# Moving pieces of prompt attention between VectorE, GpSimd and ScalarE, with one rotation and one transposed tile for q and k

## The chip, the cores and the metric

The kernel runs on one core of a Trainium2 chip. The metric is device time in microseconds (us) of one launch, the median of a few runs. TensorE multiplies, VectorE (DVE), ScalarE (ACT) and GpSimd (POOL) do the elementwise work, and SyncE (SP) issues most of the transfers. Each engine works through its own instructions in the order in which the program lists them: an instruction that waits holds up everything behind it on its engine.

## The reference

One inference step of a hybrid decoder layer, in float32: 2048 prompt tokens and 32 sample tokens (8 sequences of 4) of width 1024.

```python
qa, ka, va, qb, kb, vb, ga, gb = _project(x, w_in)
qa, ka, qb, kb = _rope(qa, pos), _rope(ka, pos), _rope(qb, pos), _rope(kb, pos)
# A: 8 query heads on 2 key heads, window 128, with sinks
oa = _band_values(_sink_softmax(_band_scores(qa, ka, 128), sink), va)
# B: three groups of 4 heads; group g reads every 1st, 4th or 16th earlier key
for g, (win, dil) in enumerate(((128, 1), (512, 4), (2048, 16))):
    qg, kg, vg = (_stride_split(z[:, :, hs], dil) for z in (qb, kb, vb))
    p, lse = _softmax_lse(_band_scores(qg, kg, win // dil))
    outs.append(_stride_merge(_band_values(p, vg), n, dil))
ob = _combine_groups(outs, lses)
mix = (sigmoid(ga) * (oa @ w_br_a) + sigmoid(gb) * (ob @ w_br_b)) @ w_o
h = layernorm(ALPHA * x + mix)
u, v = split(h @ w_up)
y = layernorm(ALPHA * h + (gelu(causal_conv3(u)) * v) @ w_down)
```

The sample tokens do the same against cached keys and values. The rotated keys and the values are outputs too.

## The kernel before, in words

**Arithmetic.** TensorE multiplies in a reduced float32 format. To keep float32 accuracy, each operand is split (`split`, lines 40 to 42): ACT copies it to the reduced format (the high half), and DVE, or POOL where the call says so, subtracts that from the original (the low half). A product is then three matmuls: high by high, low by high, high by low.

**Phases.** Phase 1 projects and does all attention; phase 2 merges the branches and applies the first norm; phase 3 is the gated feed-forward. The change lies in phase 1 alone.

**Phase 1.** It runs through five stages: B0, B1, B2 (the three groups of branch B, with strides of 1, 4 and 16 tokens between the rows of a tile), A, and G (the rest of the gates). A stage has 16 prompt tiles of 128 tokens and one sample tile. Each tile has a **slot** (`slot`, line 352): 96 matmuls of 256 columns in two halves, each half into a PSUM tile of the pool `pd`, which has two buffers. A half is four blocks of weights in two steps each, so a slot has eight steps (u, kh). After every step, `adv` lets each pending attention job do its next piece, the newest job first; then the weights of the next stage may be split (`adv_w`), and at steps (1,0) and (3,0) `adv_bg` does one piece of the sample scores.

In a B slot the pieces come so (numbers are steps of the slot after the tile's own projection):

- (0,0): `attn_b` begins. Two transposes of q into a PSUM tile of pool `psT` (three buffers), two of k into one of pool `psO` (one buffer), then `split_q` (ACT L589, DVE L591) and `split_k` (ACT L604 and L606, DVE L608). After it the job before does its last piece: the values of the second pair of heads (L659, into `psT`), their evacuation `both` (ACT L570, DVE L571), an addition on POOL (L662) and a store issued on POOL (L663).
- (0,1): `split_v`. Then `prep`: in B0, `trans_x` transposes the next tile of x through two `psT` tiles (L335) into R, which holds x transposed; in all stages `make_xs` splits the next tile's columns of R (ACT L41, then the low half, L42). In B1 and B2 these columns are read with a stride of 4 or 16 elements.
- (1,0): scores (L617, L619) and `softmax_pair` (line 541): the masked maximum on DVE (L546), its scaling `nm` on DVE (L550), the exponentials on ACT (L552); then a store of maxima and denominators, issued on POOL (L644), which waits for the last exponential. Then `adv_bg`: in `sample_scores` (line 766) DVE multiplies the cached keys by the sample's queries (L797) and sums over the head dimension (L800).
- (2,1): transposes of the first probabilities (L562) and their split (PT, L41 and L42); then, late by design, `evac` of the slot's first half: the rotation `rope` of q and k (L425, L426, L433), which is the last reader of that half's `pd` tile.
- (3,0): the second probabilities; `adv_bg` again, with a product and its sum.
- (3,1): the values of the first pair of heads (L659, into `psO`) and their evacuation.

A tile of a pool is given the buffer that was given out longest ago, and its first writer waits until the last reader of what was there is done. In a B0 slot six `psT` tiles are taken, in this order: q's transposes, the earlier job's values, the two of `trans_x`, and two of transposed probabilities.

In stage A the slot has the same eight steps, `attn_a` has four score tiles per slot, its scaling is at L698, and the low half of the next tile is on POOL already. Products of the sample scores of B0, B1 and B2 run in stages B1, B2 and A: sixteen each, in B1 and B2 two per slot.

What the profile calls `pst` are transposes, `psd` the projections, `pso` values, `xs` the split columns of x, `w` weights, `b` general buffers.

Of the kernel before, what the change touches and what calls it, by code (L numbers as in the profile page):

```python
# [7 lines left out]
F32 = mybir.dt.float32  # L8
F32R = mybir.dt.float32r
AF = mybir.ActivationFunctionType  # L10
ALU = mybir.AluOpType
# [6 lines left out]
NS = 32  # L18
# [6 lines left out]
SCALE = HD ** -0.5  # L25
# [9 lines left out]
class Net:  # L35
# [142 lines left out]
    def phase1(self):  # L178
        nc, tc, a = self.nc, self.tc, self.a
        with ExitStack() as st:  # L180
# [42 lines left out]
            for n, (kind, i, t) in enumerate(seq):  # L223
# [6 lines left out]
                nextp = [q for q in seq[n + 1:n + 3] if q[1] < 16][:1]  # L230
# [9 lines left out]
                def prep():  # L240
                    if kind == "B0" and i + 1 < 16:
                        if i + 2 < 16:
                            self.load_x(i + 2)
                        self.trans_x(i + 1)
                        if i == 0:
                            self.load_xs()
                        if i == 1:
                            self.xs_sample()
                    if nextp and nextp[0][0] != "G" and t[0] == "p":
                        self.load_cs(nextp[0][2][1])  # L250
                    if t[0] == "p" and nextp:
                        return self.make_xs(nextp[0][2], kind == "A")
                    return None

                x2 = self.slot(kind, i, t, xs, units, prep, after_unit, rp)
# [197 lines left out]
    def evac(self, kind, i, t, half, ps):  # L453
        nc, a = self.nc, self.a
        rows = t[1]
        if kind == "G":
            self.gate_out(kind, t, ps, 1024 + half * 512, 512, rows)
            return
        if half == 0:
            cs = self.cs = self.css.pop(0)  # L460
            q = self.at1.tile([128, 512], F32, tag="q", name="q")
            kv = self.at1.tile([128, 512], F32, tag="kv", name="kv")
            self.q, self.kv = q, kv
            if kind == "A":
                self.rope([(q.rearrange("p (r s d) -> p s r d", r=4, s=2), 0, 8)], ps, cs, 128, 8)
            else:
                self.rope([(q[:, 0:256].rearrange("p (h d) -> p h d", d=64), 0, 4),
                           (kv[:, 0:256].rearrange("p (h d) -> p h d", d=64), 4, 8)], ps, cs, 128, 8)
            return
        kv = self.kv  # L470
        if kind == "A":
            self.rope([(kv[:, 0:128].rearrange("p (h d) -> p h d", d=64), 0, 2)], ps[:, 0:128], self.cs, 128, 2)
            self.vr = self.split_v(ps[:, 128:256])
        else:
            self.vps = ps[:, 0:256]
            if kind == "B2" or i == 15 or (kind == "B1" and i % 4 == 3):
                nc.scalar.activation(kv[:, 256:512], ps[:, 0:256], AF.Copy)
            if kind == "B0" and i == 15:
                nc.gpsimd.dma_start(a["cache_b1_p"], kv)
            elif kind == "B1" and i % 4 == 3:  # L480
                nc.gpsimd.dma_start(a["cache_b2_p"][i // 4:i // 4 + 509:4, :], kv)
            elif kind == "B2":
                nc.gpsimd.dma_start(a["cache_b3_p"][rows, :], kv)
        self.gate_out(kind, t, ps[:, 256:512], self.gcol[kind][0] * 256, 256, rows)
        if kind == "A" and i == 15:
            v = self.buf()
            nc.scalar.activation(v[:, 0:128], ps[:, 128:256], AF.Copy)
            nc.gpsimd.dma_start(a["cache_a_p"][:, 0:128], kv[:, 0:128])
            nc.gpsimd.dma_start(a["cache_a_p"][:, 128:256], v[:, 0:128])

    def evac_sample(self, kind, half, ps):
# [9 lines left out]
        if half == 0:  # L501
            self.cs_s = self.at.tile([NS, 128], F32, tag="cs", name="css")
            nc.sync.dma_start(self.cs_s, a["c_rope"][rows, :])
            q = self.at1.tile([NS, 512], F32, tag="q", name="sq")
            kv = self.buf(NS)
            self.q, self.kv = q, kv
            if kind == "A":
# [33 lines left out]
    def softmax_pair(self, sps, nk, mask, m, nm, den, cols, accum=True, init=None):  # L541
# [5 lines left out]
                out=P[:, x, :nk], in0=sps[:, x * 256:x * 256 + nk], in1=mask, scale=1.0,  # L547
                scalar=NEG if init is None else init[:, c:c + 1], op0=ALU.add, op1=ALU.max, accum_out=m[:, c:c + 1])
        csl = slice(cols[0], cols[1] + 1, cols[1] - cols[0])
        nc.vector.tensor_scalar(nm[:, csl], m[:, csl], -SCALE, None, ALU.mult)  # L550
        for x, c in enumerate(cols):
            nc.scalar.activation(P[:, x, :nk], P[:, x, :nk], AF.Exp, bias=nm[:, c:c + 1], scale=SCALE,  # L552
                                 accum_out=den[:, c:c + 1])
# [68 lines left out]
    def attn_b(self, kind, i, t):  # L622
# [3 lines left out]
        sl, mask, nb, swap = self.keys(i, has_prev)  # L626
        nk = nb * 128
        ps = self.psT.tile([128, 512], F32, tag="t", name="pst")
        for p in range(2):
            nc.tensor.transpose(ps[:, p * 128:(p + 1) * 128], q[:, p * 128:(p + 1) * 128], self.idn)  # L630
        qT = self.split_q(ps[:, 0:256].rearrange("p (r t) -> p r t", r=2))
        ps = self.psO.tile([128, 512], F32, tag="o", name="pst")
        for p in range(2):
            nc.tensor.transpose(ps[:, p * 128:(p + 1) * 128], kv[:, p * 128:(p + 1) * 128], self.idn)
        self.split_k(ps[:, 0:256].rearrange("p (r t) -> p r t", r=2), i % 2)
        yield
        v = self.split_v(self.vps)
        vprev, self.vprev = self.vprev, v
# [27 lines left out]
    def attn_a(self, t):  # L666
# [22 lines left out]
        def softmax(r, x, sps):  # L689
# [4 lines left out]
            for y in range(2):  # L694
                nc.vector.tensor_tensor_reduce(out=P[:, y, :nk], in0=sps[x][:, y * 256:y * 256 + nk], in1=mask, scale=1.0,
                                               scalar=self.sk8[:, c + y:c + y + 1], op0=ALU.add, op1=ALU.max,
                                               accum_out=m[:, c + y:c + y + 1])
            nc.vector.tensor_scalar(nm[:, c:c + 2], m[:, c:c + 2], -SCALE, None, ALU.mult)  # L698
            for y in range(2):
                nc.scalar.activation(P[:, y, :nk + 1], P[:, y, :nk + 1], AF.Exp, bias=nm[:, c + y:c + y + 1], scale=SCALE,  # L700
                                     accum_out=den[:, c + y:c + y + 1])
# [64 lines left out]
    def sample_scores(self, g):  # L766
# [25 lines left out]
        for n, (b, th) in enumerate(steps):  # L792
# [1 line left out]
            if n + 1 < len(steps):  # L794
                nxt = load(*steps[n + 1])
            q3 = qb.rearrange("p (t c) -> p t c", t=Kv.shape[1])
            nc.vector.tensor_tensor(q3, Kv, q3, ALU.mult)  # L797
            c0 = b * 4 + th * 2
            dst = self.S[:, g, :, c0:c0 + 2]
            nc.vector.tensor_reduce(dst.rearrange("p h t -> p t h"), qb.rearrange("p (t h d) -> p t h d", t=2, d=64), AX.X, ALU.add)  # L800
# [832 lines left out]
```

## Time and profile before

| | |
|---|---|
| runs | 3258.58, 3260.72 and 3261.48 us, median 3260.72 |
| profiled execution | 3259.99 us, of which the span from first to last instruction is 3258.2 |
| busy | TensorE 3175.0 us (97%), DVE 1947.6 (60%), ACT 1397.0 (43%), POOL 565.5 (17%) |
| stages | B0 to about 280 us, B1 to 535, B2 to 790, A to 1085, G to 1340, phase 2 to 1712, phase 3 to the end |

The span starts with the first instruction. A matmul's row gives its pipelined duration, so consecutive ones overlap. "Idle before" is the time in which an engine stood still before an instruction, with the instruction that ended the wait.

### The profile page before, as it was taken

What the parts mean: (1) busy time and instruction counts of PE and PEld (TensorE: products, weight loads), DVE (VectorE), ACT (ScalarE), POOL (GpSimd) and SP (SyncE); (2) the same over time, 40 slices, a digit from 0 to 9 for tenths busy, and PEclk for the clock granted to TensorE, in tenths of its full rate; (3) what the DMA queues carried; (4) which work ended last, traced back from release to release, by engine and by line L of the source; (5) the groups of instructions that cost most, each with busy time, mean ns of one, the idle gap of its engine ahead of it and who ended that gap; (6) DMA issues with size and microseconds to landing.
All of it is one profiled execution on the core that took longest, in us unless ns stands there. A gap on an engine that the chain in (4) does not pass through costs nothing.

```text
span 3258.2 us, 56718 instructions
## 1 busy us (share of the span) xinstructions
PE 3175.0 (97%) x21839; PEld 2907.4 (89%) x21839; DVE 1947.6 (60%) x4030; ACT 1397.0 (43%) x3097; POOL 565.5 (17%) x671
## 2 busy tenths in 40 slices
PE   8999999999999899899999999999999999999999
PEld 8998999999899899788877988888888888999998
DVE  5667877877887632577765444564446444574446
ACT  6666656665666533412224243342243332342332
POOL 2112112223121200255540000030002100030001
PEclk9999999999999999999999999999999999999999
DMA  3113212412221343876744323443334423443231
GB/s 116 56 47 95 82 31 86 121 63 89 79 57 38 91 131 98 227 194 175 187 131 140 121 84 101 127 142 91 95 100 120 139 86 101 120 138 91 69 95 57
DMA packets 480036, 343.02 MB, mean 105 GB/s; under 512 B 113938, under 2 KB 435564, under 8 KB 479766
## 3 DMA queue, kind: packets, MB, share of 16 engines
q1 hardware_dynamic: 462390, 290.78, 31.5%
q0 software_dynamic: 17232, 48.56, 4.8%
q8 instruction: 172, 2.82, 0.4%
q14 instruction: 98, 0.80, 0.1%
q10 hardware_dynamic: 144, 0.07, 0.0%
HBM read 279.71 MB, written 59.59 MB: 104 GB/s over the span
## 4 chain that ended last, share of the span: by engine, by line
PE 58%; issue 2%; DMA 2%; DVE 1%; SPq 0%; ACT 0%; POOL 0%; DVEq 0%; POOLq 0%; ACTq 0%
PE psu L1392 31%; PE psdn L1070 14%; PE psw L1070 5%; PE psb L1070 4%; PE psd L379 2%; PE psdf L1070 1%; DMA oa<-d_oa 1%; PE pst L1234 0%; PE pso L964 0%; PE pst L1269 0%; DMA ob<-d_ob 0%; DMA ga<-d_gate 0%; DMA b<-in_w_o 0%; SPq L1126 0%; DMA b<-in_w_br_b 0%
## 5 line engine op out<-in xcount | busy, mean ns | idle before, releaser
L1392 PE MATMUL psu<-h,w 128*128 128x512 f32 (+1 forms) x5280 | 1013.6, 354 | 2.2 <-ACT h L41 2.0
L379 PE MATMUL psd<-w,xs 128*128 128x256 f32 x7680 | 1001.1, 285 | 8.7 <-ACT w L41 4.0
L1392 PEld LDWEIGHTS psu<-h,w 128*128 128x128 f32 x5280 | 861.2, 188 | 149.0 <-ACT h L41 3.4
L379 PEld LDWEIGHTS psd<-w,xs 128*128 128x128 f32 x7680 | 945.7, 190 | 12.9 <-ACT w L41 4.4
L1070 PE MATMUL psdn<-w,gt 128*128 128x256 f32 (+1 forms) x4008 | 474.9, 279 | 2.2 <-DVE y L1443 2.2
L1070 PEld LDWEIGHTS psdn<-w,gt 128*128 128x128 f32 (+1 forms) x4008 | 472.2, 186 | 5.3 <-DVE y L1443 4.5
L42 DVE TENSOR_TENSOR w<-b,w 128x512 fp32r<-128x512 f32 (+1 forms) x613 | 403.7, 717 | 21.4 <-ACT w L41 20.4
L41 ACT ACTIVATE w<-b 128x512 fp32r<-128x512 f32 x636 | 346.5, 607 | 127.4 <-PE psdn L1070 64.2
L1403 ACT ACTIVATE ext<-psu 128x512 f32<-128x512 f32 (+1 forms) x110 | 56.3, 512 | 452.2 <-PE psu L1392 452.1
L1416 DVE SCALAR_TENSOR_TENSOR ac<-ext,cw,ac 128x512 f32<-128x512 f32 (+1 forms) x88 | 71.1, 808 | 286.9 <-ACT ac L1415 286.9
L1443 DVE SCALAR_TENSOR_TENSOR y<-y,psdn 128x256 f32<-128x256 f32 x176 | 73.2, 420 | 274.2 <-PE psdn L1070 270.4
L1070 PE MATMUL psw<-WO,mT 128*128 128x512 f32 (+1 forms) x800 | 189.4, 395 | 0.9 <-DVE mT L42 0.9
L1070 PEld LDWEIGHTS psw<-WO,mT 128*128 128x128 f32 (+1 forms) x800 | 148.5, 186 | 38.9 <-DVE mT L42 1.1
L1412 POOL COPY mix<-ext 128x2 f32<-128x2 f32 x66 | 13.0, 196 | 926.5 <-ACT ext L1403 906.4
L42 DVE TENSOR_TENSOR xs<-R,xs 128x1024 fp32r<-128x1024 f32 x64 | 104.8, 1638 | 114.9 <-ACT xs L41 114.8
L1070 PE MATMUL psb<-w,oT 128*128 128x512 f32 (+1 forms) x600 | 147.6, 404 | 7.7 <-ACT b L449 5.0
L41 ACT ACTIVATE gt<-ac 128x512 fp32r<-128x512 f32 x110 | 58.3, 549 | 222.2 <-DVE ac L1423 162.7
L1070 PEld LDWEIGHTS psb<-w,oT 128*128 128x128 f32 (+1 forms) x600 | 112.4, 190 | 36.3 <-ACT b L449 5.7
L552 ACT ACTIVATE P<-P,nm 128x256 f32<-128x256 f32 (+1 forms) x192 | 86.4, 451 | 123.1 <-issue 87.4
L42 DVE TENSOR_TENSOR PT<-pst,PT 128x512 fp32r<-128x512 f32 (+1 forms) x160 | 96.2, 608 | 66.6 <-ACT PT L41 66.0
L662 POOL TENSOR_TENSOR b<-b 64x256 f32<-64x256 f32 x96 | 71.3, 742 | 337.4 <-DVE b L571 337.4
L41 ACT ACTIVATE xs<-R 128x1024 fp32r<-128x1024 f32 x80 | 116.2, 1452 | 0.9 <-ACT b L756 0.4
(257 smaller groups left out, 3679.1 us busy)
## 6 DMA issues: line engine op xcount, KB each, us to landing
b<-in_w_up SPq DMA_DIRECT2D x352, 256.0 KB, 3.9
b<-in_w_down SPq DMA_DIRECT2D x160, 256.0 KB, 3.4
b<-in_w_in SPq DMA_DIRECT2D x80, 256.0 KB, 4.1
b<-in_x_prompt SPq DMA_DIRECT2D x64, 256.0 KB, 4.0
b<-in_cache_b SPq DMA_DIRECT2D x64, 256.0 KB, 3.3
ga<-d_gate SPq DMA_DIRECT2D x32, 512.0 KB, 5.4
b<-d_q SPq DMA_DIRECT2D x48, 256.0 KB, 3.9
d_gate<-b SPq DMA_DIRECT2D x64, 128.0 KB, 1.9
```

The costliest lines, as they stand in the source:

```text
L41: self.nc.scalar.activation(hi, src, AF.Copy)
L42: (eng or self.nc.vector).tensor_tensor(lo, src, hi.bitcast(F32), ALU.subtract)
L379: nc.tensor.matmul(dst, lhsT=l, rhs=r[:, k, :], start=(k == 0 and q == 0), stop=(k == 7 and q == len(ops) - 1))
L552: nc.scalar.activation(P[:, x, :nk], P[:, x, :nk], AF.Exp, bias=nm[:, c:c + 1], scale=SCALE, accum_out=den[:, c:c + 1])
L662: nc.gpsimd.tensor_tensor(o[:, :, 0], o[:, :, 0], o[:, :, 1], ALU.add)
L1070: self.nc.tensor.matmul(ps[:x.shape[1]], lhsT=x, rhs=w, start=(first and q == 0), stop=(last and q == len(ops) - 1))
L1392: nc.tensor.matmul(ps[:, :b1 - b0], lhsT=w[:, k, c0:c0 + 128], rhs=h[:, x, k, b0:b1], start=(k == 0 and q == 0), stop=(k == 7 and q == 2))
L1403: nc.scalar.activation(ext[:, 2 + b0:2 + e1], ps[:, 0:e1 - b0], AF.Copy)
L1412: nc.gpsimd.tensor_copy(carry[:, j, :], ext[:, W:W + 2])
L1416: nc.vector.scalar_tensor_tensor(ac[:, :L], ext[:, 1:1 + L], cw[:, 1, j:j + 1], ac[:, :L], ALU.mult, ALU.add)
L1443: nc.vector.scalar_tensor_tensor(y[x][:M, cs], y[x][:M, cs], ALPHA if first else 1.0, ps[:M], ALU.mult, ALU.add)
```

## The change

1. The low half of the next tile's columns (`make_xs`) is subtracted on POOL when the running slot is of B1, B2 or A; before, of A alone. B0 and G keep it on DVE.
2. In `softmax_pair` and in `attn_a` the scaled maxima `nm` are made by an ACT activation instead of a DVE `tensor_scalar`.
3. In B stages q and k lie side by side in one SBUF tile (`qkv`), and `rope` does both at once: one L425 and one L433 of 512 columns for two of 256 each.
4. In `attn_b` the two transposes of k go into the same `psT` tile as those of q, instead of a `psO` tile. `split_q` and `split_k` both read it.
5. The product of the sample scores (L797) is done on POOL; its sum (L800) stays on DVE.

```diff
-                        return self.make_xs(nextp[0][2], kind == "A")
+                        return self.make_xs(nextp[0][2], kind != "B0" and kind != "G")
...
-            q = self.at1.tile([128, 512], F32, tag="q", name="q")
-            kv = self.at1.tile([128, 512], F32, tag="kv", name="kv")
-            self.q, self.kv = q, kv
+            t = self.at1.tile([128, 1024], F32, tag="qkv", name="qkv")
+            q = t[:, 0:512] if kind == "A" else t[:, 256:512]
+            self.q, self.kv = q, t[:, 512:1024]
...
-                self.rope([(q[:, 0:256].rearrange("p (h d) -> p h d", d=64), 0, 4),
-                           (kv[:, 0:256].rearrange("p (h d) -> p h d", d=64), 4, 8)], ps, cs, 128, 8)
+                self.rope([(t[:, 256:768].rearrange("p (h d) -> p h d", d=64), 0, 8)], ps, cs, 128, 8)
...
-            q = self.at1.tile([NS, 512], F32, tag="q", name="sq")
+            q = self.at1.tile([NS, 1024], F32, tag="qkv", name="sq")[:, 0:512]
...
-        nc.vector.tensor_scalar(nm[:, csl], m[:, csl], -SCALE, None, ALU.mult)
+        nc.scalar.activation(nm[:, csl], m[:, csl], AF.Copy, scale=-SCALE)
...
-        for p in range(2):
-            nc.tensor.transpose(ps[:, p * 128:(p + 1) * 128], q[:, p * 128:(p + 1) * 128], self.idn)
+        for p in range(4):
+            nc.tensor.transpose(ps[:, p * 128:(p + 1) * 128], (q, kv)[p // 2][:, p % 2 * 128:(p % 2 + 1) * 128], self.idn)
         qT = self.split_q(ps[:, 0:256].rearrange("p (r t) -> p r t", r=2))
-        ps = self.psO.tile([128, 512], F32, tag="o", name="pst")
-        for p in range(2):
-            nc.tensor.transpose(ps[:, p * 128:(p + 1) * 128], kv[:, p * 128:(p + 1) * 128], self.idn)
-        self.split_k(ps[:, 0:256].rearrange("p (r t) -> p r t", r=2), i % 2)
+        self.split_k(ps[:, 256:512].rearrange("p (r t) -> p r t", r=2), i % 2)
...
-            nc.vector.tensor_scalar(nm[:, c:c + 2], m[:, c:c + 2], -SCALE, None, ALU.mult)
+            nc.scalar.activation(nm[:, c:c + 2], m[:, c:c + 2], AF.Copy, scale=-SCALE)
...
-            nc.vector.tensor_tensor(q3, Kv, q3, ALU.mult)
+            nc.gpsimd.tensor_tensor(q3, Kv, q3, ALU.mult)
```

## The prediction

> **What bounds the kernel now.** I read the stretches first: busy time of each engine by stage. Columns: stretch, its length, busy us (instructions) of TensorE, its weight loads, DVE, ACT and POOL, then granted clock, DMA share, GB/s. The rows are B0, B1, B2 and A.
>
> ```profile
> 12.00:280.00 268.00, 263.05 (x2200) 260.37 (x2198) 171.80 (x441) 166.45 (x409) 51.91 (x72) 0.99 0.24 74
> 280.00:535.00 255.00, 240.25 (x1978) 232.00 (x1976) 192.29 (x456) 153.72 (x369) 50.13 (x71) 1.00 0.21 64
> 535.00:790.00 255.00, 244.34 (x1974) 237.19 (x1975) 195.41 (x484) 155.82 (x401) 63.28 (x89) 0.97 0.31 94
> 790.00:1085.00 295.00, 286.58 (x2294) 270.49 (x2294) 233.05 (x597) 177.04 (x533) 60.73 (x48) 1.00 0.22 60
> ```
>
> TensorE sets the time everywhere: DVE is at most 79% busy. All that the change can win is TensorE's idle time in these stages: 5, 15, 11 and 8 us, plus late starts of weight loads. So the waits of TensorE, stage by stage, are next (us in total, times, longest): B1, then B2, then A.
>
> ```profile
> PE pst L634 <- DVE b L571: 6.9, 9, 0.9
> PE psd L379 <- DVE b L426: 1.8, 1, 1.8
> ...
> PEld pst L562 <- ACT P L552: 7.9, 20, 0.9
> ```
>
> ```profile
> PE pst L634 <- DVE b L571: 4.6, 9, 0.5
> PE psd L379 <- DVE b L426: 1.6, 1, 1.6
> ...
> PEld pst L562 <- ACT P L552: 3.1, 10, 0.4
> ```
>
> ```profile
> PE pso L713 <- DVE PT L42: 3.6, 14, 0.3
> PE pst L678 <- DVE kv L433: 2.5, 5, 0.6
> ```
>
> Three causes: k's transposes wait for the one `psO` buffer (L634), those of the probabilities for late exponentials (L562), and at a stage's first slot the projection waits for the rotation to free its `pd` buffer (L379 behind L426).
>
> **Gains.** (1) With k in q's tile the wait for `psO` goes: 6.9 + 4.6 = **11.5 us**. (2) The low half of x stands on DVE ahead of the maxima; without it the exponentials come about 2 us earlier, and only ACT's own high half is ahead of them. The L562 waits go; they show at the weight loads (7.9 + 3.1 = 11.0), a part of which lies under the matmul before. Between 0 and 11.0 I take **8 us**, near the top because these loads stand right ahead of TensorE's next work. (3) The same low half delays the first rotation of B1 and of B2; off DVE, 1.8 + 1.6 = **3.4 us** go. (4) In A, DVE loses a product per step (the L797 row below) and the scaling, which POOL's low half holds up in every slot:
>
> ```profile
> 899.32 1.40 DVE L698 TENSOR_SCALAR nm<-m 128x2 f32<-128x2 f32 x1
> ```
>
> ```profile
> L693 ACT ACTIVATE P<-sk 128x2 f32<-128x2 f32 x64 | 12.6, 196 | 0.0
> ```
>
> On ACT a form of the same size takes 0.196 us (L693), so the scaling costs ACT 0.2 us, is no longer held, and the exponentials of A come about 1.2 us earlier. A's two waits, 3.6 + 2.5 = 6.1 us, are mostly covered; I take **5.5 us** (bounds 0 and 6.1). (5) The rotation at once issues two instructions fewer per tile, but consecutive DVE instructions overlap (starts 0.33 us apart, below), so it gains under 0.1 us per tile, and none of it ends a wait of TensorE: 0. The 160 scalings on ACT, 0.2 us each, lie under ACT's 38% idle in these stages: 0. Sum: 11.5 + 8 + 3.4 + 5.5 = **28.4 us**.
>
> **A loss in B0.** In each B0 slot six `psT` tiles are taken on three buffers, so the second tile of `trans_x` gets the buffer of q's transposes. Its last reader is now L591; with k in the same tile it becomes L608, the last part of `split_k`. One slot of B0 (start, duration):
>
> ```profile
> 138.34 0.86 DVE L591 TENSOR_TENSOR qT<-pst,qT 64x256 fp32r<-64x256 f32 x2 [1.07 <-ACT qT L589]
> ...
> 139.50 1.03 PE L335 MATMUL pst<-idn,b 128*128 128x128 f32 x8
> 139.93 0.87 DVE L608 TENSOR_TENSOR kL<-pst,kH 64x256 fp32r<-64x256 f32 x2 [0.73 <-ACT kH L606]
> ```
>
> L591 ends at 139.20; the fifth of the eight transposes, the first into the second tile, starts at 139.93 without a wait. L608 ends at 140.80, and a handoff from DVE to TensorE takes 0.06 us (669.98 + 0.67 to 670.71 below), so this transpose could start at 140.86: TensorE stands still for 0.93 us, in a slot that has no idle time to absorb it. L608 can't come earlier, since ACT's L606 ends its wait. Slots 2 to 14 of B0 have the same order: 13 x 0.93 = **12.1 us**. Bounds: 0, if the wait is kept by columns rather than by buffer, and 13 x 1.14, if ACT's first copy waits for all four transposes, two more of about 0.1 us each (1.03 for eight).
>
> **A new wait in B1 and B2.** In a slot with a product, POOL's order becomes: store of values (L663), low half of x, store of maxima (L644, which waits for the exponentials), product. DVE's order is: sum L800, then PT, then the rotation. So the sum stands on DVE waiting for POOL, and PT and the rotation behind it; and the rotation's L426 frees the `pd` buffer of the next slot's first matmul. A slot of B2:
>
> ```profile
> 669.98 0.67 DVE L571 TENSOR_TENSOR b<-pso,b 64x512 f32<-64x512 f32 x1
> ...
> 670.71 0.44 PE L634 MATMUL pst<-idn,kv 128*128 128x128 f32 x2 [0.52 <-DVE b L571]
> ...
> 673.71 2.01 ACT L41 ACTIVATE xs<-R 128x1024 fp32r<-128x1024 f32 x1
> ...
> 675.39 0.73 POOL L663 DMA_DIRECT2D d_ob<-b  x1 [0.30 <-POOL b L662]
> ...
> 678.97 0.69 DVE L797 TENSOR_TENSOR b<-b 128x512 f32<-128x512 f32 x1
> 679.69 0.69 DVE L800 TENSOR_REDUCE S<-b 128x8 f32<-128x512 f32 x1
> 680.38 0.56 POOL L644 DMA_DIRECT2D d_md<-md  x1 [4.27 <-ACT PT L41]
> 680.39 0.42 DVE L42 TENSOR_TENSOR PT<-pst,PT 128x256 fp32r<-128x256 f32 x1
> 680.73 0.41 DVE L425 TENSOR_TENSOR q<-psd,cs 128x256 f32<-128x256 f32 x1
> 681.06 0.41 DVE L425 TENSOR_TENSOR kv<-psd,cs 128x256 f32<-128x256 f32 x1
> 681.39 0.68 DVE L426 TENSOR_TENSOR b<-psd,cs 128x512 f32<-128x512 f32 x1
> 682.83 1.58 PE L379 MATMUL psd<-w,xs 128*128 128x256 f32 x12
> ```
>
> Durations on POOL, contiguous and strided on DVE (B0, B1, A on POOL, and a POOL `tensor_tensor` of the product's size; min/median/max):
>
> ```profile
> L42 DVE TENSOR_TENSOR xs<-R,xs x16: 1224/1226/2029, 24.6 to 251.3; 128x1024 fp32r<-128x1024 f32 x16
> L42 DVE TENSOR_TENSOR xs<-R,xs x14: 1961/2032/2048, 312.2 to 514.0; 128x1024 fp32r<-128x1024 f32 x14
> L42 POOL TENSOR_TENSOR xs<-R,xs x15: 2382/2394/2409, 802.9 to 1069.5; 128x1024 fp32r<-128x1024 f32 x15
> L1221 POOL TENSOR_TENSOR m<-ga x34: 1267/1303/1642, 1344.1 to 1693.5; 128x512 f32<-128x512 f32 x32, 32x512 f32<-32x512 f32 x2
> ```
>
> The product is 1.30 us. The low half takes 2.39 on POOL contiguous; strided by 4 or 16 elements it is unknown, call it d. DVE pays 2.03 - 1.23 = 0.80 for the stride. Bounds: 2.39 (POOL too slow to notice) and 2.39 x 2.03 / 1.23 = 3.95; I take the same addition as DVE's, **3.2**, since it is the same operation on the same memory.
>
> Then: POOL is free at 675.39 + 0.73 = 676.12 (ACT's high half ends at 675.72). Low half, store, product and sum with three handoffs: 676.12 + d + 0.56 + 1.30 + 0.69 + 0.18 = 678.85 + d. PT (0.34 to the next start), L425 (0.66), L426 (0.68) and the handoff: 680.59 + d. The next slot's matmul, now at 682.83, would come at 682.31 without the 0.52 us at L634. Wait: **d - 1.72**. The exponentials aren't the limit: the store that waits for them stands at 680.38 now, they come about 2 us earlier, and POOL's low half ends at 679.3.
>
> A B1 slot with two key blocks has a longer PT and more work on TensorE. From one without a product, whose L562 wait (0.66, and 0.93 - 0.60 in the four transposes) goes too:
>
> ```profile
> 496.42 2.08 ACT L41 ACTIVATE xs<-R 128x1024 fp32r<-128x1024 f32 x1
> 498.08 0.73 POOL L663 DMA_DIRECT2D d_ob<-b  x1 [0.29 <-POOL b L662]
> 502.19 0.93 PE L562 MATMUL pst<-idn,P 128*128 128x128 f32 x4 [0.66 <-ACT P L552]
> 504.12 0.69 DVE L42 TENSOR_TENSOR PT<-pst,PT 128x512 fp32r<-128x512 f32 x1 [1.79 <-ACT PT L41]
> 504.39 0.60 PE L562 MATMUL pst<-idn,P 128*128 128x128 f32 x4
> 506.71 1.58 PE L379 MATMUL psd<-w,xs 128*128 128x256 f32 x12
> ```
>
> 498.81 + d + 2.73, then 0.61 + 0.66 + 0.68 + 0.06, is 503.55 + d against 505.72: **d - 2.17**. Sixteen slots hold products: six of B1 with two key blocks, two with one, eight of B2 with one. At 3.2: 6 x 1.03 + 10 x 1.48 = **21.0 us**; at 2.39: 8.0; at 3.95: 33.0.
>
> [...]
>
> **The sum.** 12.1 + 21.0 - 28.4 = +4.7 us on the profiled execution's own 3259.99 us (span 3258.2, 1.8 around it): **3265 us**. That execution lies 0.7 under the median of the runs, 3260.72. 0.2% is 6.5 us, what a measurement here tells from no change: 3265 counts as the same.
>
> **Rivals.**
>
> *The stride costs POOL nothing* (d = 2.39). For it: POOL needs 2.39 us where DVE needs 1.23, so its reads may have slack. Against: ACT and DVE both pay. New wait 8.0: 12.1 + 8.0 - 28.4 = -8.3, **3252 us**.
>
> *B0 does not wait*: the second tile of `trans_x` finds its buffer free. For it: nothing in the trace shows this reuse, since no wait falls there now. Against: L634's wait for L571 shows that a PSUM buffer waits for its last reader. 3265 - 12.1 = **3253 us**.
>
> *The chain on POOL is longer still*, the case that ends slower: in the sixteen slots POOL pays for the stride in DVE's proportion, d = 3.95; new wait 33.0, sum +16.7, **3277 us**. It makes the kernel slower than the measurement's 0.2% from d = 3.3 on.
>
> *POOL's product shuts out the rotation's second half.* A DVE operation stood still for as long as POOL's low half ran (L698, 1.40 us). The second product (1.30 us) ends, by the times above, about 1 us before the rotation's additions L433 begin. If it ran 1.3 us later, L433 and q's transposes behind it would be late by up to 0.5 us in sixteen slots: +8, **3273 us**. [...]
>
> **How the numbers follow.** Chances: forecast (d from 2.9 to 3.6, 3260 to 3271) 0.42; no cost of the stride 0.20; no wait in B0 0.13; longer chain 0.15; rotation shut out 0.10. The forecast's 0.42 is same 0.30 and slower 0.12; the two rivals at 3252 and 3253 are faster for two thirds (0.22) and same for the rest (0.11); the last two are slower (0.25). So faster 0.22, same 0.41, slower 0.37. The range, 3247 to 3281, spans the rivals with some 4 us beyond, for the takes of 8 and 5.5.
>
> **What would show it.** B0: TensorE waiting at L335 for L608, about 0.95 us in 13 slots, and slots of 16.4 us; without it the loss is wrong. B1 and B2: no wait at L634 nor L562; in slots with products a wait at L379 for L426 of 1 to 1.5 us, and DVE idle ahead of L800 until POOL. The strided low half on POOL: 3.2 us; 2.4 or 4 decides between the cases. A: slots about 0.3 to 0.9 us shorter. If the L379 wait is absent though d is over 3, the order I read from the queues is wrong.

## The result and the profile after

The changed kernel takes 3304.68 us (median; 3299.81 to 3306.83) beside 3261.10 (3258.58 to 3261.72) of the kernel before on the same chip: a ratio of 1.0133, 95% interval 1.0115 to 1.0151. It is 44 us slower; the prediction was 3265, with a range up to 3281. Its profiled execution took 3304.76 us (span 3303.0).

The stretches of the changed kernel first, cut at the same distances from each stage's first transposes of q as those shown of before, to within a microsecond (length, busy time and instructions of TensorE, weight loads, DVE, ACT, POOL; granted clock, DMA share, GB/s):

```profile
12.00:320.00 308.00, 273.07 (x2196) 267.08 (x2196) 164.95 (x376) 174.16 (x440) 51.95 (x71) 0.97 0.21 65
320.00:581.70 261.70, 249.72 (x1984) 237.37 (x1982) 142.48 (x361) 160.79 (x402) 117.54 (x103) 1.00 0.21 62
581.70:855.60 273.90, 253.22 (x1973) 239.71 (x1974) 147.62 (x389) 163.47 (x434) 129.41 (x121) 0.99 0.28 88
855.60:1133.60 278.00, 276.42 (x2296) 270.47 (x2297) 195.17 (x521) 187.78 (x593) 81.51 (x64) 1.00 0.23 64
```

TensorE, idle for 5 us of B0 before, now stands still for 35 us there, and its clock is 0.97. In A it is hardly idle at all. From the first transposes of q of one stage to those of the next (start times in the trace; A to those of its sixteenth tile), the stages of the profiled executions are:

| us | B0 | B1 | B2 | A | the rest |
|---|---|---|---|---|---|
| before | 262.9 | 262.6 | 243.7 | 282.6 | 2206.4 |
| changed | 303.7 | 269.2 | 262.7 | 265.6 | 2201.8 |
| difference | +40.8 | +6.6 | +19.0 | -17.0 | -4.6 |

What TensorE waits for in B0 of the changed kernel (us in total, times, longest; "issue" means that the profile names nothing that ended the wait):

```profile
PE pst L335 <- issue: 25.7, 13, 2.2
...
PE pst L343 <- ACT R L336: 2.0, 1, 2.0
```

The wait that the prediction foretold for B0 is there, 13 times, but it is 1.96 us long instead of 0.93. One such slot (start, duration):

```profile
157.63 0.60 PE L629 MATMUL pst<-idn,qkv 128*128 128x128 f32 x4
158.27 0.77 ACT L588 ACTIVATE qT<-pst 64x256 fp32r<-64x256 f32 x2 [0.85 <-PE pst L629]
...
159.07 0.86 DVE L590 TENSOR_TENSOR qT<-pst,qT 64x256 fp32r<-64x256 f32 x2 [1.29 <-ACT qT L588]
...
159.96 0.77 ACT L603 ACTIVATE kH<-pst 64x256 fp32r<-64x256 f32 x2 [0.93 <-DVE qT L590]
...
160.74 0.78 ACT L605 ACTIVATE kH<-pst 64x256 fp32r<-64x256 f32 x2
161.55 0.86 DVE L607 TENSOR_TENSOR kL<-pst,kH 64x256 fp32r<-64x256 f32 x2 [1.63 <-ACT kH L605]
...
162.51 0.63 PE L335 MATMUL pst<-idn,b 128*128 128x128 f32 x4 [1.95 <-issue]
```

L335 starts 0.10 us after L607, the last reader of the buffer, has ended (161.55 + 0.86 = 162.41). The row to see is ACT L603. It copies k out of the shared tile and needs nothing of `qT`, yet it waits 0.93 us until DVE has subtracted q's low half (L590: 159.07 + 0.86 = 159.93). So ACT and DVE read the tile (the expectations call it a bank) in turns: ACT q, DVE q, ACT k, DVE k. The turns are kept by semaphores of the program: in the trace this L603 waits for the one that the second L590 raises. In the slot of before that the prediction shows, ACT's first copies of k waited for TensorE's semaphore alone and ran beside DVE's L591 (138.34):

```profile
137.12 0.38 PE L630 MATMUL pst<-idn,q 128*128 128x128 f32 x2
...
138.33 0.77 ACT L604 ACTIVATE kH<-pst 64x256 fp32r<-64x256 f32 x2
```

There k's low half ended 3.68 us after the transposes began (140.80 - 137.12); now it is 4.78 (162.41 - 157.63), and the buffer is free only then. It is so in all 48 B slots; for L603 the trace has this wait (us, times):

```profile
  DVE qT L590: 44.9, 48
```

In B1 (first list) and B2 (second) it shows at the scores, whose weight loads (PEld) wait for k's halves (L616, L618):

```profile
PE psd L379 <- DVE b L426: 4.9, 8, 0.8
...
PEld pss L618 <- DVE kL L607: 8.6, 32, 0.3
PEld psd L379 <- PE pso L655: 6.3, 8, 1.0
...
PEld pss L616 <- ACT kH L605: 2.5, 8, 0.9
```

```profile
PE psd L379 <- DVE b L426: 6.3, 8, 0.8
...
PEld pss L618 <- DVE kL L607: 8.6, 32, 0.3
PEld psd L379 <- PE pso L655: 8.0, 9, 1.0
...
PEld pss L616 <- ACT kH L605: 5.0, 18, 1.1
```

The waits for `psO` at k's transposes and those for late exponentials (L634 and L562 of before) are gone from both lists, as foretold. In their place stand the scores' 24.7 us (8.6 + 2.5 + 8.6 + 5.0) and, in slots with a product, the wait at L379. Such a slot of B1:

```profile
436.35 2.91 POOL L42 TENSOR_TENSOR xs<-R,xs 128x1024 fp32r<-128x1024 f32 x1
...
439.20 0.56 POOL L640 DMA_DIRECT2D d_md<-md  x1
439.77 2.55 POOL L793 TENSOR_TENSOR b<-b 128x512 f32<-128x512 f32 x2
...
441.11 0.69 DVE L796 TENSOR_REDUCE S<-b 128x8 f32<-128x512 f32 x1 [4.87 <-POOL b L793]
441.71 0.68 DVE L42 TENSOR_TENSOR PT<-pst,PT 128x512 fp32r<-128x512 f32 x1
...
442.91 0.68 DVE L426 TENSOR_TENSOR b<-psd,cs 128x512 f32<-128x512 f32 x1
443.73 1.66 PE L379 MATMUL psd<-w,xs 128*128 128x256 f32 x12 [0.56 <-DVE b L426]
```

The chain is the predicted one, link by link: low half, store, product, sum, PT, rotation, matmul. The strided low half takes 2.91 us where the prediction took 3.2.

### The profile page after: what moved, and what is told of

Same layout as the page of the kernel before. It is cut to its first block, busy times and chain, and to the rows that moved or that the text cites. A ratio compares the mean times of both kernels' runs of the same rounds, so it can differ in the third digit from the quotient of the medians.

```text
span 3303.0 us, 56625 instructions
## 1 busy us (share of the span) xinstructions
PE 3192.0 (97%) x21839; PEld 2921.9 (88%) x21839; DVE 1804.3 (55%) x3694; ACT 1430.3 (43%) x3257; POOL 721.8 (22%) x751
## 4 chain that ended last, share of the span: by engine, by line
PE 60%; DMA 1%; DVE 1%; issue 1%; ACT 0%; POOL 0%; SPq 0%; DVEq 0%; ACTq 0%; POOLq 0%
PE psu L1388 30%; PE psdn L1066 14%; PE psw L1066 5%; PE psb L1066 4%; PE psd L379 4%; PE psdf L1066 1%; DMA oa<-d_oa 1%; PE pso L960 1%; PE pst L1230 0%; PE pst L1265 0%; DMA ob<-d_ob 0%; DVE w L42 0%; DMA b<-in_w_o 0%; DVE y L1439 0%; DMA b<-in_w_br_a 0%
## 5 line engine op out<-in xcount | busy, mean ns | idle before, releaser
L379 PE MATMUL psd<-w,xs 128*128 128x256 f32 x7680 | 1004.4, 285 | 19.9 <-DVE b L426 11.5
L379 PEld LDWEIGHTS psd<-w,xs 128*128 128x128 f32 x7680 | 946.9, 190 | 27.4 <-PE pso L655 14.3
L41 ACT ACTIVATE PT<-pst 128x512 fp32r<-128x512 f32 (+1 forms) x160 | 84.3, 536 | 124.3 <-PE pst L561 123.4
L42 POOL TENSOR_TENSOR xs<-R,xs 128x1024 fp32r<-128x1024 f32 x48 | 132.3, 2757 | 22.9 <-ACT xs L41 13.3
```

The lines of the kernel that those rows point to most:

```text
L41: self.nc.scalar.activation(hi, src, AF.Copy)
L42: (eng or self.nc.vector).tensor_tensor(lo, src, hi.bitcast(F32), ALU.subtract)
L379: nc.tensor.matmul(dst, lhsT=l, rhs=r[:, k, :], start=(k == 0 and q == 0), stop=(k == 7 and q == len(ops) - 1))
```

## The experiments

Each ratio is against runs of the kernel before on the same chip. Stage lengths are worked out as in the table above, from one profiled execution each; what lies outside the four stages comes to between 2201.0 and 2212.4 us there, so sums over the stages differ from differences of the medians by up to some 7 us.

| kernel | us, median | ratio, 95% interval | B0 | B1 | B2 | A |
|---|---|---|---|---|---|---|
| changed, k in its own tile again | 3234.60 | 0.9920 (0.9905 to 0.9935) | 262.2 | 253.8 | 245.2 | 265.6 |
| before, k in q's tile alone | 3328.27 | 1.0208 (1.0192 to 1.0223) | 304.3 | 277.8 | 261.2 | 282.7 |
| changed, ACT's copies first | 3261.87 | 1.0006 (0.9997 to 1.0015) | 281.3 | 256.3 | 249.9 | 265.6 |
| changed, x through the scores' tile | 3288.25 | 1.0084 (1.0068 to 1.0101) | 283.0 | 269.2 | 262.9 | 265.7 |
| changed, x through the values' tile | 3275.45 | 1.0047 (1.0030 to 1.0064) | 270.3 | 269.1 | 263.5 | 265.6 |
| changed, product on DVE | 3288.21 | 1.0084 (1.0069 to 1.0100) | 303.7 | 261.0 | 251.5 | 266.1 |
| before, product on POOL alone | 3294.15 | 1.0109 (1.0094 to 1.0124) | 262.9 | 276.0 | 262.1 | 284.5 |
| the same, store of maxima on ACT | 3270.26 | 1.0031 (1.0020 to 1.0042) | 263.9 | 266.2 | 251.8 | 284.2 |
| before, low half on POOL alone | 3244.95 | 0.9951 (0.9937 to 0.9966) | 262.1 | 254.2 | 237.8 | 283.0 |
| before, scaling on ACT alone | 3247.30 | 0.9957 (0.9940 to 0.9973) | 263.0 | 264.1 | 245.4 | 266.1 |
| changed, k own tile, product on DVE | 3222.12 | 0.9886 (0.9871 to 0.9900) | 262.2 | 250.3 | 236.5 | 266.2 |
| changed, k in a scores' tile, product on DVE | 3222.03 | 0.9881 (0.9865 to 0.9897) | 262.0 | 247.2 | 237.3 | 266.2 |

**1. k back in its own tile**, the rest of the change as it is.

```diff
-        for p in range(4):
-            nc.tensor.transpose(ps[:, p * 128:(p + 1) * 128], (q, kv)[p // 2][:, p % 2 * 128:(p % 2 + 1) * 128], self.idn)
+        for p in range(2):
+            nc.tensor.transpose(ps[:, p * 128:(p + 1) * 128], q[:, p * 128:(p + 1) * 128], self.idn)
         qT = self.split_q(ps[:, 0:256].rearrange("p (r t) -> p r t", r=2))
-        self.split_k(ps[:, 256:512].rearrange("p (r t) -> p r t", r=2), i % 2)
+        ps = self.psO.tile([128, 512], F32, tag="o", name="pst")
+        for p in range(2):
+            nc.tensor.transpose(ps[:, p * 128:(p + 1) * 128], kv[:, p * 128:(p + 1) * 128], self.idn)
+        self.split_k(ps[:, 0:256].rearrange("p (r t) -> p r t", r=2), i % 2)
```

> The changed kernel, with k's transposes back in their own psO tile and all else kept. Bank theory: B0 as before the change, the scores of B1 and B2 no longer wait for k, stage A keeps its gain of 17 us; what is left of the loss is the rotation behind the sum in the sixteen slots with products, 10 to 16 us by the forecast's formula with the measured 2.9 us low half; 3240 to 3258 us. POOL theory: only the 12 us of B0 come back; about 3292 us.

Measured: 3234.60, 70 us below the changed kernel and 0.8% below the one before, better than the 3240 to 3258 expected. B0, B1 and B2 lose 41.5, 15.4 and 17.5 us, 74.4 together. Two rows of its B0 show ACT's copies of k and DVE's subtraction of q starting together again:

```profile
138.36 0.77 ACT L603 ACTIVATE kH<-pst 64x256 fp32r<-64x256 f32 x2
138.37 0.86 DVE L590 TENSOR_TENSOR qT<-pst,qT 64x256 fp32r<-64x256 f32 x2 [1.07 <-ACT qT L588]
```

So the tile that q and k share costs more than the whole loss; the other four parts together are a gain.

**2. The shared tile alone**, put into the kernel before (the edit is the first one's reverse).

> The kernel before, with only the two transposes of k moved into the PSUM tile of q. Bank theory (ACT and DVE read one PSUM bank only in turn, so splitting q and splitting k run one after the other, k's low half comes 1.1 us later in each B slot, and in B0 the second tile of x waits for it about 2 us in 13 slots): B0 longer by 35 to 42 us as in the changed kernel, the waits for the psO buffer (11.5 us) gone in B1 and B2 but scores and exponentials about 0.6 us later there; 3290 to 3310 us. POOL theory (the loss comes from the queue of low half, store, product and sum): B0 longer by my predicted 12 us at most, B1 and B2 shorter by 11; 3262 us.

Measured: 3328.27, worse than expected by either theory. Against before, B0, B1 and B2 gain 41.4, 15.2 and 17.5 us, 74.1 together. These are the same sizes as in the first experiment, so the expectation's discount for the other parts was wrong: over the stages the shared tile costs 74 us whether they are there or not (by the medians 70 there and 67 here). TensorE waits 25.7 us at L335 here too, the same as in the changed kernel, which clears POOL for B0.

**3. ACT's copies first.** q and k stay in one tile and in the same buffers; ACT copies both high halves before DVE subtracts, and k's second copies come from SBUF.

```diff
         for x, here, there in self.HALF:
             nc.scalar.activation(qT[x][here, :n], q3[here], AF.Copy)
-        for x, here, there in self.HALF:
-            nc.vector.tensor_tensor(qT[x][there, :n], q3[here], qT[x][here, :n].bitcast(F32), ALU.subtract)
...
         for x, here, there in self.HALF:
             nc.scalar.activation(self.kH[x][here, :n, cur], k3[here], AF.Copy)
         for x, here, there in self.HALF:
-            nc.scalar.activation(self.kH[x][there, :n, cur], k3[here], AF.Copy)
+            nc.scalar.activation(self.kH[x][there, :n, cur], self.kH[x][here, :n, cur].bitcast(F32), AF.Copy)
+        for x, here, there in self.HALF:
+            nc.vector.tensor_tensor(qT[x][there, :n], q3[here], qT[x][here, :n].bitcast(F32), ALU.subtract)
         for x, here, there in self.HALF:
             nc.vector.tensor_tensor(self.kL[x][here, :n, cur], k3[here], self.kH[x][here, :n, cur].bitcast(F32), ALU.subtract)
```

> The changed kernel, q and k in one bank and in the same buffers; only the order in the splits differs: ACT copies the high halves of q and k out of the bank first (four reads), takes k's second copies from SBUF, and DVE then does its four subtractions. So the bank changes hands once instead of three times. Bank theory: DVE's first subtraction starts about 0.8 us later than now (after ACT's fourth read), but k's low half ends about 1.2 us earlier; the wait at L335 falls from 25.7 to some 10 us, the half-clock stretches of B0 go, the waits of L616 and L618 for k fall to under 5 us: B0 275 to 285, total 3265 to 3280. Rival (k is late for another reason, and ACT and DVE may read one bank at once): DVE's subtraction of q starts right behind ACT's copies of q as now, k's low half gains under 0.3 us: 3300 to 3306.

Measured: 3261.87, 43 us below the changed kernel by the order of ten small instructions and the source of two, and the same as before. A slot of its B0 (L606 are the first copies of k, L608 those from SBUF, L611 and L613 the subtractions):

```profile
145.15 0.60 PE L635 MATMUL pst<-idn,qkv 128*128 128x128 f32 x4
145.78 0.77 ACT L588 ACTIVATE qT<-pst 64x256 fp32r<-64x256 f32 x2 [0.85 <-PE pst L635]
146.57 0.78 ACT L606 ACTIVATE kH<-pst 64x256 fp32r<-64x256 f32 x2
147.25 0.84 ACT L608 ACTIVATE kH<-kH 64x256 fp32r<-64x256 f32 x2
...
147.38 0.86 DVE L611 TENSOR_TENSOR qT<-pst,qT 64x256 fp32r<-64x256 f32 x2 [2.09 <-ACT kH L606]
...
148.25 0.86 DVE L613 TENSOR_TENSOR kL<-pst,kH 64x256 fp32r<-64x256 f32 x2
...
149.21 0.63 PE L335 MATMUL pst<-idn,b 128*128 128x128 f32 x4 [1.14 <-issue]
```

L611 subtracts q and has its operands at 146.55, but starts at 147.38, when ACT has read k out of the same tile (146.57 + 0.78 = 147.35): the rival, by which both read it at once, falls. L608, which reads SBUF, runs beside L611 (147.25 to 148.09, and from 147.38). The low half of k ends 3.96 us after the transposes began (4.78 in the changed kernel), a gain of 0.82, not the expected 1.2. The wait at L335 falls to 1.14 us, 15.0 in all where some 10 were expected, and those of the scores' weight loads for k in B1 and B2 from 24.7 to 6.8 in all. The total is below the expected 3265 to 3280.

**4. Which part of B0's loss is the late buffer?** The second tile of `trans_x` is taken elsewhere, so L335 has nothing to wait for; q and k keep sharing. First from the scores' pool, then from the values'.

```diff
-            ps = self.psT.tile([128, 512], F32, tag="t", name="pst")
+            ps = (self.psS if h else self.psT).tile([128, 512], F32, tag="s" if h else "t", name="pst")
```

> The changed kernel, with one edit: the second of the two tiles in which trans_x transposes the next tile of x (stage B0 alone) comes from the pool of the scores, so it no longer needs the buffer in which q and k lie. q and k stay in one bank. It tells apart two parts of B0's loss of 41 us: the buffer handed on late (L335 behind L607) and k's late low half as such. Theory 1 (most of B0 is the buffer): the 25.7 us at L335 go, the slots lose their 2.1 us and the half-clock windows with them, B0 comes to 265 to 275, B1 and B2 stay at 269 and 263: 3304.8 - 34 = about 3270 (3266 to 3277). Theory 2 (B0's loss is the late k; the wait at L335 only stands where the scores would wait otherwise): scores then wait at L616 and L618, B0 stays above 285: 3287 or more.

Measured: 3288.25, which lies in the second theory's range; B0 283.0, which neither theory gave. The wait at L335 is gone, but a new one took its place, because the scores' second buffer now waits for the copy of x out of it:

```profile
PE pss L616 <- ACT R L336: 15.1, 14, 1.4
```

So the run doesn't decide. The second, with `psO` and tag "o" in place of `psS` and "s":

> The changed kernel; the second tile of trans_x (B0 alone) comes from the pool of the values (psO), which stands empty at that time. q and k stay in one bank. With the scores' pool the wait at L335 went, but 15.1 us came at L616, behind the copy of x out of the scores' buffer (B0 283.0). Here nothing should come in its place. Theory 1 (B0's loss is the buffer handed on late, and the half clock that its waits bring): B0 263 to 267, 3264 to 3270. Theory 2 (k's late low half costs B0 something of its own): B0 270 to 283, 3271 to 3287. B1 and B2 stay at 269 and 263 by both.

Measured: 3275.45; B0 270.3, and no wait took the old one's place. Both numbers lie in the second theory's ranges, B0 at their lower edge, yet both theories hold a share: 33.4 us of B0 go with the buffer, and 7.4 over before's 262.9 stay with the late k. Slots of B0 here last 15.88 us, against 15.47 in the first experiment, with hardly any idle time of TensorE; the row that differs is the weight loads' wait for the probabilities, 6.8 us in all (0.8 in the first experiment):

```profile
PEld pst L561 <- ACT P L551: 6.8, 27, 0.8
```

**5. Product back on DVE**, otherwise the changed kernel.

```diff
-            nc.gpsimd.tensor_tensor(q3, Kv, q3, ALU.mult)
+            nc.vector.tensor_tensor(q3, Kv, q3, ALU.mult)
```

> The changed kernel, with the product of the sample scores back on DVE. If the waits of the projection for the rotation come from the sum that stands behind POOL's product: they go (11 us of TensorE idle, and about 1.2 us per B2 slot with products), B1 and B2 shorter by 12 to 18 us, 3286 to 3293 us. If they come from the low half of x on POOL or from k's bank alone: within 3 us of 3305 us.

Measured: 3288.21, 16.5 us less, as expected (B1 8.2, B2 11.2); the waits at L379 behind L426 are gone. In the weight loads' rows they came to 14.3 us (the rows that name L655 above: 6.3 and 8.0), now 0.4; the wait of the values for PT, on the same chain, falls from 10.8 to 5.1. Together these fell by 19.6 us, close to the 19.4 by stages.

**6. Product on POOL alone**, in the kernel before: does it cost anything without the low half ahead of it?

> The kernel before with the fifth part alone: the product of the sample scores on POOL, the low half of x on DVE. By the prediction's chain, wait = d - 1.72 with d = 0 on POOL: no new wait at L379; the store of maxima, later by the low half's 2 us on DVE, adds some: 3259 to 3264. Rival: the product costs what it cost beside POOL's low half (12 to 16 us), since POOL and DVE hold each other up in SBUF: 3270 or more.

Measured: 3294.15, a miss: it costs 34 us, twice as much as in the changed kernel (B1 +13.4, B2 +18.4). A slot of B2:

```profile
592.23 0.56 POOL L644 DMA_DIRECT2D d_md<-md  x1 [4.20 <-ACT PT L41]
592.85 2.52 POOL L797 TENSOR_TENSOR b<-b 128x512 f32<-128x512 f32 x2
...
594.17 0.69 DVE L800 TENSOR_REDUCE S<-b 128x8 f32<-128x512 f32 x1 [3.36 <-POOL b L797]
...
596.60 1.66 PE L379 MATMUL psd<-w,xs 128*128 128x256 f32 x12 [0.85 <-DVE b L426]
```

POOL stands idle for 4.20 us at the store of the maxima, and the product behind it (the row names PT, ACT's next instruction; the last exponential ends at 591.94). With the low half on DVE the exponentials that the store waits for come late. I had put d = 0 into the prediction's sum and forgotten that the store then sets the time.

**7. The same, with the store of the maxima issued on ACT.**

```diff
-        nc.gpsimd.dma_start(self.d_md[g, rows, :], md)
+        nc.scalar.dma_start(self.d_md[g, rows, :], md)
```

> The kernel before with the product on POOL (which alone gave 3294) and one edit more: the store of maxima and denominators is issued on ACT, right behind the exponentials that it waits for, instead of on POOL ahead of the product. Theory 1 (the product is late because that store stands ahead of it on POOL and waits 4 to 5 us for the exponentials, and the sum on DVE waits for the product): the wait of DVE at L800 (56.5 us in B1 and B2) falls under 10, the waits at L379 behind L426 go, B1 and B2 come back to 263 and 244 or some us less, 3254 to 3264. Theory 2 (POOL's product, two operands from SBUF, holds DVE up by itself, or is held up): the loss stays above 12 us in B1 and B2, 3272 or more.

Measured: 3270.26, between the two ranges. DVE's wait at the sum is gone altogether, as the first theory says, and 20 of the 32 us with it. B1 and B2 still stand 3.6 and 8.1 over before, which the second theory explains in kind:

```profile
593.34 1.96 DVE L42 TENSOR_TENSOR xs<-R,xs 128x1024 fp32r<-128x1024 f32 x1 [0.97 <-ACT xs L41]
...
593.84 3.80 POOL L797 TENSOR_TENSOR b<-b 128x512 f32<-128x512 f32 x2
...
596.88 0.79 DVE L550 TENSOR_SCALAR nm<-md 128x2 f32<-128x2 f32 x1
```

Freed of the store, the pair of products (2.52 us above) starts during DVE's low half (first row) and takes 3.80, and the scaling of a 128x2 tile takes 0.79 us, not the 0.17 that it takes before (mean of 32 in B2: 0.453 against 0.172). This one ends at 597.67, POOL's pair at 597.64. It is so for all 32 scalings of B1 and B2 that took over 0.3 us here: each ends 0.02 to 0.03 us after one of POOL's products. So the two engines held each other up in these slots (3.80 us for 2.52, 0.79 for 0.17), and the exponentials wait for the scaling. That this is all of the 11.7 us left was not tried; the edit has a price of its own, since ACT computes nothing for up to 0.40 us around the issue of the store (0.33), which comes to 11.2 us in B1 and B2.

**8. The low half on POOL alone**, in the kernel before.

```diff
-                        return self.make_xs(nextp[0][2], kind == "A")
+                        return self.make_xs(nextp[0][2], kind != "B0" and kind != "G")
```

> The kernel before with the first part alone: the low half of the next tile's columns on POOL in B1 and B2. Products stay on DVE, k in its own tile. By the gains as the prediction sized them (waits at L562, 11.0 us, of which 8; the first rotations, 3.4) B1 and B2 are about 11 us shorter: 3250 (3248 to 3252). Rival: the waits at L634 and L562 are one chain, and what is saved at L562 comes back at L634, since the values that free the buffer come no earlier: under 4 us, 3257 to 3261.

Measured: 3244.95, better than the 3248 to 3252 expected; B1 and B2 lose 8.4 and 5.9 us. The rival falls.

**9. The scaling on ACT alone**, in the kernel before (the change's second part).

> The kernel before, with only the scaling of the maxima moved to ACT. If A's gain of 17 us comes from the scaling that stood behind POOL's low half: A shorter by 10 to 17 us, B stages within 2 us, 3244 to 3251 us. If it comes from DVE losing the products: A shorter by 5 us at most, 3256 us or more.

Measured: 3247.30, as expected for a gain in A: A loses 16.5 us, B1 and B2 nothing (+1.5, +1.7). The weight loads of A before, and below of this run, show where it sat (L562 is gone from the second list):

```profile
PEld pso L713 <- DVE PT L42: 9.6, 27, 0.5
PEld pst L562 <- ACT P L700: 7.7, 29, 0.5
PEld pst L678 <- DVE kv L433: 3.7, 5, 0.8
```

```profile
PEld pso L713 <- DVE PT L42: 3.1, 13, 0.2
...
PEld pst L678 <- DVE kv L433: 1.5, 5, 0.4
```

The three rows fall from 21.0 us to 4.6, by 16.4. In the kernel before, 15 of A's scalings took 0.84 to 1.89 us, and each ended 0.02 to 0.04 us after POOL's low half; on ACT the scaling waits for POOL no longer.

**10. Without the two parts that cost**: k in its own tile and the product on DVE; then the same with k's transposes in a tile of the scores' pool, as stage A does it.

> The changed kernel with k's transposes back in their own tile (as in the run that gave 3234.6) and the product back on DVE. If the product on POOL costs what it cost beside the shared bank (16.5 us, there with 12.6 us of waits of L379 behind L426), this comes to 3218 to 3222. If with its own bank only the waits at L379 matter (6.5 us in that run), 3226 to 3230.

> The changed kernel with k's transposes in a tile of the scores' pool, as stage A does it, and the product on DVE. q and k in separate banks, and no wait for the one buffer of the values' pool (L633 behind L570, 6.7 us with k there). If that buffer is all that is left between this and the run with k in the values' pool: 5 to 7 us below that one, 3212 to 3222. Rival: the scores' tiles are reused by k, so that the scores of the next pair of heads wait for split_k or k waits for the maxima and exponentials of the job before: then no better than that run, 3220 to 3235.

Measured: 3222.12 and 3222.03, 1.1 to 1.2% faster than the kernel before. Taking the product off POOL is worth 12.5 us here by the medians (12.2 by stages), more than its waits at L379 (6.5) and less than the 16.5 beside the shared tile. The two kernels can't be told apart: the wait for `psO` goes (B1 is 3.1 us shorter), but with k in the scores' pool the total is no better, and 3222 is where the first expected range ends and inside the rival's. The trace shows the rival's first wait: in B1 and B2 the scores' weight loads (L616) wait 6.5 us in all there, where k's transposes waited 9.2 us with k in its own tile.

## Why the prediction was wrong

By its own steps, in us over the stages B0 to A:

| term | predicted | measured | from |
|---|---|---|---|
| k in q's tile: B0, less the waits at L634 | 12.1 - 11.5 = +0.6 | +74.4 | experiment 1 |
| product on POOL behind the low half | +21.0 | +12.2 | experiment 10, first run, to experiment 1 (B1 3.5, B2 8.7) |
| low half off DVE (8 + 3.4) | -11.4 | -14.3 | experiment 8 |
| A | -5.5 | -17.0 | stage table |
| scaling, one rotation in B1 and B2 | 0 | -5.2 | experiment 8 to the first run of 10 (the scaling alone: +3.2) |
| B0 without the shared tile | 0 | -0.7 | before to experiment 1 |
| sum, B0 to A | +4.7 | +49.4 | stages: 40.8 + 6.6 + 19.0 - 17.0 = 49.4 |

With -4.6 in the other stages this is the +44.8 between the profiled executions. The rows are steps of one path from before to the changed kernel, so they add up by their making; rows of a few us, the scaling's and the 4.6 among them, may be no more than the difference between single executions. The terms depend on the kernel in which they are measured: beside the shared tile the product costs 19.4 (experiment 5), in the kernel before 31.8 (experiment 6).

**The step that failed** is the term for k in q's tile: the sentence "L608 can't come earlier, since ACT's L606 ends its wait", and the sum built on it, which leaves L608 where it was; only the upper bound of 1.14 asks whether it comes later. It replayed the splits as they ran in two tiles, q's subtraction on DVE beside k's copies on ACT. In one tile they take turns. That makes k's low half 1.1 us later (4.78 us after the first transposes instead of 3.68). The wait in B0 was 1.96 us instead of 0.93; the term, put at +0.6 us with the gain at L634, measured +74.4. My upper bound of 13 x 1.14 allowed 0.2 us for two more transposes and nothing for the reads themselves. And it counted the delay in B0's buffer alone, not in the scores of the other 32 slots.

The prediction didn't weigh that ACT and DVE both read the shared tile. Their turns stand in the traces, as 0.93 us at L603 (44.9 in the 48 B slots) and 2.09 at L611 in experiment 3: the part of the change that looked like a pure saving, one tile for two, was the one to check for it.

**B0, +40.8.** The mechanism was right (the second tile of `trans_x` gets the buffer of q and k) and 13 waits came. They last 1.96 us: 25.7 us. A second wait of the kind, 2.0 us at L343, I had not counted. A third term was not in the prediction at all, the clock. Three neighbouring slots of the changed kernel, each from the start of its wait at L335 to the next, columns as above:

```profile
123.87:141.45 17.58, 15.62 (x133) 15.41 (x132) 9.25 (x22) 10.13 (x27) 2.74 (x4) 1.00 0.15 50
141.45:160.56 19.11, 17.15 (x133) 16.94 (x132) 9.34 (x22) 10.13 (x27) 2.75 (x4) 0.91 0.15 47
160.56:178.13 17.57, 15.62 (x133) 15.41 (x132) 9.25 (x22) 10.12 (x27) 2.74 (x4) 1.00 0.14 39
```

In five of the slots that wait, the granted clock drops like this, and they last 19.1 us instead of 17.6: 7.5 us. Together 35.2; the late probabilities (experiment 4: 7.4 with the buffer out of the way) bring it to 42.6, near the 40.8. The parts come from different kernels, so the match is a rough one.

**B1 and B2, +25.6 instead of -1.9.** The waits at L634 and L562 went, and the wait at L379 came, as foretold, for the reason foretold. With d at its measured 2.91 the prediction's own formula gives 6 x 0.74 + 10 x 1.19 = 16.3 us; taking the product off POOL gave 16.5 in the medians, 19.4 by stages. That the sizes agree is in part luck: the formula prices TensorE's wait at L379, and that wait was 11.2 us (4.9 + 6.3); the rest of the cost sat at weight loads that it did not price. The stride costs POOL 2.91 against 2.39 contiguous, between the lower bound and the value taken. No run shows the 3.6 us that the forecast's d goes up to: the strided low half took 2.91, with a median of 2.91 in B1 and in B2. What turned the sign is the shared tile: 32.9 us of experiment 1 lie in these two stages. There the weight loads stand idle for 58.5 us in the changed kernel and for 35.2 in experiment 1, which explains 23 of them; where the rest lies is not shown.

**A, -17.0 instead of -5.5.** The cause was named and the size was wrong. I bounded the gain by TensorE's idle time there, 6.1 us. The three rows of experiment 9 add up to 21.0 us of late starts at the weight loads; 16.4 of them go with the scaling, and A loses 16.5. So late weight loads held the matmuls up without showing as idle time of TensorE.

**The rivals.** That B0 does not wait, and that the stride is free, both fell. The case that ends slower was slower for another reason than its own. POOL and DVE did hold each other up, but at the scaling, which the change itself had moved to ACT (on DVE up to 0.79 us beside the product in experiment 7 and up to 1.89 beside the low half in the kernel before, 0.17 otherwise). The rotation's second half, L433, met no product: 46 of its 48 take 0.69 us, and the two that met POOL's low half, at the ends of B0 and B1, 1.96 and 1.98.

## What to carry to other kernels

Before putting two operands into one PSUM tile, list who reads it. Here ACT and DVE both did, and their reads came one after the other: the change of hands at L603 held ACT up for 44.9 us in the 48 B slots, on the path of everything that waits for the last part. Letting ACT read first took 43 us off the changed kernel (experiment 3), keeping two tiles 70 (experiment 1). And to size a wait that goes, read the weight loads' rows too: in A they held 21.0 us where TensorE's own two waits came to 6.1. To size work that moves to another engine, look for a store ahead of it on that engine's queue that waits for something unrelated: in experiment 6 it held the product up for 4.20 us in the slot shown.

## What the runs showed of the hardware

In the changed kernel the turns are taken over the whole tile. ACT's two copies L588 cover partitions 0 to 63 and 64 to 127, and DVE's subtraction of the first half begins at 159.07, only when both are done (158.27 + 0.77 = 159.04). In the trace only the second copy raises the semaphore that DVE waits for, so this order is the program's. Whether the chip would let the two engines read it at once, no run shows.

In B0 of the changed kernel TensorE was put to half clock, though none of its waits between 12 and 320 us was longer than 2.2 us. The trace records the granted clock in stretches that begin on one grid of 3.41 us. Two neighbouring stretches of the grid in the changed kernel (columns as above):

```profile
141.20:144.61 3.41, 1.45 (x14) 1.24 (x13) 1.94 (x5) 3.23 (x9) 0.60 (x1) 1.00 0.18 61
144.61:148.03 3.42, 3.42 (x19) 3.42 (x18) 1.67 (x4) 1.12 (x2) 0.86 (x2) 0.50 0.15 43
```

The first holds a whole wait at L335 (1.96 us from 141.45 on); in the next the clock is 0.50. Of the thirteen waits at L335 the five that put 1.95 us or more into one stretch of the grid were each followed by a stretch at 0.50. The eight that a border of the grid divides, with at most 1.88 us on one side, were not. So among these thirteen it went with the place of the wait on the grid which slots lost 1.5 us. The wait at L343, with 1.84 us on one side, was followed by one, so these figures give no exact limit. With waits of 1.14 us at the same place (experiment 3) B0 shows none:

```profile
12.00:297.00 285.00, 263.63 (x2196) 258.65 (x2197) 165.99 (x376) 172.94 (x438) 52.30 (x70) 1.00 0.22 69
```

The scaling on DVE, of a 128x2 tile, was held while POOL worked: it took up to 0.79 us beside POOL's product (experiment 7), 0.84 to 1.89 in fifteen slots of A beside POOL's low half (the kernel before; 1.40 in the one that the prediction shows), and ended within 0.04 us of POOL's instruction each time. The median of A's 64 is 0.170.
